# Expert routing of a two-layer block: when key lists are searched, when their sums run, and how a spilled table is fetched back

## The chip, the cores and the metric

The kernel runs on one core of one Trainium2 chip. The metric is device time in microseconds (us) of that core, from start to end of one execution; smaller is better. One core has TensorE (PE, with its weight loads shown apart as PEld), VectorE (DVE), ScalarE (ACT), GpSimd (POOL) and SyncE (SP), each with its own instruction queue, and 16 DMA engines that all queues share.

## The reference

512 tokens of width 1024 go through a first transformer block and then a second one. The change lies in the last part of the second block, a layer of 16384 experts that is addressed by product keys (PEER):

```python
q = (xn @ wq).reshape(bsz, s, PEER_HEADS, 2, PEER_HALF)
sub = jnp.einsum('bshpd,hpnd->bshpn', q, subkeys)       # 8 heads x 2 halves x 128 keys
s_top, i_top = lax.top_k(sub, PEER_TOPK)                # best 16 keys of each half
cand = (s_top[..., 0, :, None] + s_top[..., 1, None, :]) # 256 sums of pairs
best, pos = lax.top_k(cand, PEER_TOPK)                  # best 16 pairs
expert = jnp.take_along_axis(cand_idx, pos, axis=-1)    # expert = 128 * i + j
gate = jax.nn.softmax(best, axis=-1)
...
a = jax.nn.gelu(jnp.einsum('td,ted->te', xb, ub))       # ub = u_tab[expert]
y = jnp.einsum('te,ted->td', gb * a, vb)                # vb = v_tab[expert]
```

So each token picks 8 x 16 = 128 experts, and its result is the sum of their rows of `v_tab`, each weighted by its gate and by the gelu of its row of `u_tab` times the token.

## The kernel before, in words

Tokens stand in four blocks (tb = 0 to 3) of 128. The kernel treats them in two ways. For the first 320 tokens (blocks 0, 1 and half of block 2) it computes **all** 16384 experts densely on TensorE, and multiplies by a matrix of gates that is zero wherever a token did not pick the expert. For the other 192 tokens it **gathers** the rows that were picked, 1024 numbers for each of 128 tokens in one gather of 512 KB, and multiplies on VectorE. All matmuls of weights work on pairs: `unit` (L132) loads 512 KB of weights into a ring of four buffers (`raw`), ScalarE rounds it into `whi` (L138), VectorE takes the rest as `wlo` (L140), and `mm3` makes three matmuls of it (L156 to L158).

The parts in order, with the names that matter here:

- **Queries.** 16 units of `peer_wq`, four at a time (loop `c4`), give for each block and half-head 128 key scores `sub`. After every four units the scores of these four half-heads are copied out.
- **Key lists.** `top_keys` (L909) finds the best 16 of 128 keys of a half-head with five VectorE instructions (L914 to L918). Blocks 2 and 3 are searched beside the queries (list `todo`); blocks 0 and 1 after `keys` of blocks 2 and 3.
- **Keys.** `keys` (L921) adds the lists' pairs, finds the best 16 of them (L940 to L945), and looks up the key numbers. The look-up runs in four steps: ScalarE copies an operand (L968), VectorE compares and multiplies (L972, L973), and TensorE sums over eight matmuls (L976; L978 too for block 2). Its end gives the row numbers `gidx2` (block 2) and `gidx` (block 3), with which the gathers begin, or the transposed gates `sTs`.
- **Gates.** `build` (L1024) makes the gate matrix from one-hot operands: VectorE L1036, L1037, L1043, TensorE L1050, ScalarE L1051, in 48 steps. The first `N_RES` = 2 of 16 groups of it stay on chip (`gres`), the others go to DRAM (`g_dram`).
- **First half.** Beside keys and gates, 100 dense `u_block`s (L872) run on TensorE: 24 matmuls with 320 columns, gelu, result into `ab` and from there to DRAM (`a_dram`), four blocks in one store of 640 KB. The other 28 `u_block`s are left for the second half. `SPAIR` lists the 50 pairs of the first half.
- **Second half.** 64 pairs: `second` (L1160) multiplies the activations of a pair by its gates (L1170) and splits them into `wvhi` and `wvlo`; `v_block` (L1176) multiplies them by two units of `peer_v`. Activations come back from `a_dram` as `al` (two pairs a load, two buffers), gates from `g_dram` as `gl` (eight expert rows, 1536 KB a load, two buffers).
- **Gathers.** `gathered` (L887) gathers 64 times for the half of block 2, 128 times `u` rows (L899) and 128 times `v` rows (L906) for block 3, with seven buffers. 

What sets the order: `route` and `gat` are Python generators. Each `yield` names a price in us, and `advance(gen, us)` runs a generator until its prices use up the budget that the main loop gives it: `TOP_US` = 5.0 a query unit, `R_US` = 3.6 a `u_block`, `G_US` = 2.3 half a pair. A framework then places each engine's instructions in its own order within what the dependences allow, so an instruction can stand before or after its place in the program text. All loads of `raw`, `al` and `gl` are issued by SP, one after the other.

Of the kernel before, what the change touches and what calls it, by code (L numbers as in the profile page):

```python
# [39 lines left out]
N_RES = 2  # L40
# [20 lines left out]
def tile_layers(ctx: ExitStack, tc: tile.TileContext, A: dict, out: bass.AP):  # L61
# [793 lines left out]
    g_dram = drp.tile([16 - N_RES, 128, 24, 8, 16], F32, name="g_dram")  # L855
    a_dram = drp.tile([32, 128, 4, N_U], F32, name="a_dram")

# [63 lines left out]
    def keys(pr, tb):  # L921
# [41 lines left out]
        pt = bank("b")  # L963
        pt2 = bank("b") if tb == 2 else None
        for a in range(2):
            for b0 in range(0, 16, 8):
                sx = pr.tile([128, 4, 128, 2], F16, name="ohh", bufs=2).rearrange("p x i t -> p (x i t)")
                S.copy(sx.rearrange("p (b h k) -> p b h k", b=8, h=8),  # L968
                       sf[:, :, a, b0:b0 + 8].rearrange("p h b -> p b h")[:, :, :, None].to_broadcast([128, 8, 8, 16]))
                eq = pr.tile([128, 4, 128, 2], F16, name="ohl", bufs=2).rearrange("p x i t -> p (x i t)")  # L970
                e3 = eq.rearrange("p (b s) -> p b s", b=8)
                V.tensor_tensor(e3, iotab[:, b0:b0 + 8], kf[:, a, None, :].to_broadcast([128, 8, 128]), op=OP.is_equal)  # L972
                V.tensor_tensor(eq, eq, sx, op=OP.mult)  # L973
                for b in range(8):
                    l, r = (ident16, e3[:, b]) if tb == 3 else (e3[:, b], ident16)
                    T.matmul(pt[:, a * 128:(a + 1) * 128], l, r, start=(b0 + b == 0), stop=(b0 + b == 15))  # L976
                    if tb == 2:
                        T.matmul(pt2[:, a * 128:(a + 1) * 128], turn16, e3[:, b], start=(b0 + b == 0), stop=(b0 + b == 15))  # L978
# [8 lines left out]
        ge = pr.tile([128, 8, 16], F32, name="ge")  # L987
        V.tensor_tensor(ge, bv, bv[:, :, 0:1].to_broadcast([128, 8, 16]), op=OP.subtract)
        S.activation(ge, ge, AF.Exp)
        gsu = small.tile([128, 8], F32, name="gsu")  # L990
        V.tensor_reduce(gsu, ge, axis=AX.X, op=OP.add)
        V.reciprocal(gsu, gsu)
        if tb == 3:
# [9 lines left out]
        V.tensor_copy(g16, sl[:, 0])  # L1003
        V.tensor_tensor(sl[:, 1], sl[:, 0], g16, op=OP.subtract)
        for j in range(2):
# [4 lines left out]
        yield 3.0  # L1010

    def weights2():

        S.activation(zg[64:128, 0:64], ga2[64:128], AF.Gelu_apprx_tanh)
        S.activation(zg[0:64, 64:128], ga2[0:64], AF.Gelu_apprx_tanh)
        zp = bank("b")[:, 0:64]
        T.matmul(zp, zg, fold, start=True, stop=True)
        V.tensor_tensor(gT2, zp, gT2, op=OP.mult)
# [42 lines left out]
    with ExitStack() as st:  # L1061
# [24 lines left out]
        nc.scalar.dma_start(skT, A["skT"])  # L1086
        todo = []

        def routed():
            while todo or not keyed:  # L1090
                if todo:
                    yield from todo.pop(0)
                else:
                    yield 0.0
            st2.close()
            pr = pool("pr", stack=st)
            yield from keys(pr, 2)
            yield from keys(pr, 3)
            for tb in (0, 1):
                yield from top_keys(sub[tb], tb, range(16))  # L1100
            for tb in (0, 1):
                yield from keys(pr, tb)
                yield from build(pr, tb)
            while not made2:
                next(gat)
            weights2()
            yield 0.5
            yield from build(pr, 2)
# [4 lines left out]
        for c4 in range(4):  # L1113
# [10 lines left out]
            for tb in range(4):  # L1124
                S.copy(sub[tb][:, c4 * 4:c4 * 4 + 4, :], sb_[tb].rearrange("p (a n) -> p a n", a=4))
            todo += [top_keys(sub[tb], tb, range(c4 * 4, c4 * 4 + 4)) for tb in (2, 3)]
        keyed.append(True)
        for n4 in range(0, 2 * len(SPAIR), 4):
            ab = ptop.tile([128, 4, N_U], F32, name="ab", bufs=2)
            for j in range(4):  # L1130
                u_block(2 * SPAIR[(n4 + j) // 2] + j % 2, ab[:, j, :], "a")
# [5 lines left out]
            nc.scalar.dma_start(a_dram[n4 // 4], ab)  # L1137
        for _ in route:
            pass

    with ExitStack() as st:
        pv = pool("pv", stack=st)
        yb_ = [[bank("a") for _ in range(2)] for _ in range(2)] + [[bank("b") for _ in range(2)]]
        state = {"debt": 0.0}

        def first(p, j):

            if j == 0:
                if p in SPAIR:
                    n = SPAIR.index(p)  # L1150
                    if n % 2 == 0:
                        state["al"] = pv.tile([128, 4, N_U], F32, name="al", bufs=2)
                        nc.sync.dma_start(state["al"], a_dram[n // 2])
                    state[p] = state["al"][:, 2 * (n % 2):2 * (n % 2) + 2, :]
                else:
                    state[p] = pv.tile([128, 2, N_U], F32, name="av", bufs=2)
            if p not in SPAIR:
                u_block(2 * p + j, state[p][:, j, :], "b")

        def second(p):  # L1160

            i1 = 2 * p
            if i1 % 8 == 0 and i1 // 8 < N_RES:
                state["gl"] = gres[i1 // 8]
            elif i1 % 8 == 0:
                state["gl"] = pv.tile([128, 24, 8, 16], F32, name="gl", bufs=2)
                nc.sync.dma_start(state["gl"], g_dram[i1 // 8 - N_RES])
            av = state.pop(p)
# [7 lines left out]
        def v_block(i1, w):  # L1176
            vu = unit(A["peer_v"][i1 * 128:(i1 + 1) * 128, :])
            for tb in range(3):
                for hf in range(2):
                    mm3(yb_[tb][hf], w[0][:, i1 % 2, tb * 128:(tb + 1) * 128], w[1][:, i1 % 2, tb * 128:(tb + 1) * 128],  # L1180
                        vu[0][:, hf * 512:(hf + 1) * 512], vu[1][:, hf * 512:(hf + 1) * 512], i1 == 0, i1 == 127)

        for j in range(2):
            first(0, j)
        w = second(0)
        first(1, 0)
        for p in range(64):
            g_us = G_US if p in SPAIR else 1.5 * G_US
            if p < 63:
                first(p + 1, 1)  # L1190
                wn = second(p + 1)
            v_block(2 * p, w)
            state["debt"] = advance(gat, state["debt"] + g_us)
# [143 lines left out]
```

## Time and profile before

| | |
|---|---|
| median of 3 runs | 2130.1 us (2130.02 to 2134.15) |
| the profiled execution | 2130.1 us, of which the span of the trace is 2128.4 us |
| PE busy | 2048.3 us, 96% |
| DVE busy | 1575.3 us, 74% |
| queries of the expert layer | about 970 to 1048 us of the span |
| first half (100 `u_block`s, keys, gates) | about 1050 to 1485 us |
| second half (64 pairs) | about 1485 to 2118 us |

The profile is of one execution. A matmul's end is modelled, so a busy PE is not PE at its peak; what counts for PE is its idle time and the granted clock (PEclk, 1.00 is 2.4 GHz, 0.5 is 1.2 GHz). A wait is put down to the instruction that released it.

### The profile page before, as it was taken

Reading aid. Unit: us, or ns where it says so; the run is one execution under the profiler, and the core shown is the slowest. Engines: PE = TensorE matmul, PEld = TensorE weight load, DVE = VectorE, ACT = ScalarE, POOL = GpSimd, SP = SyncE. Lnnn points to the kernel's source line nnn. Section 1 sums busy time; section 2 is a strip of 40 time slices with the busy share of each in tenths; the row PEclk is TensorE's granted clock in tenths of the full one; section 3 lists DMA queues with packets and bytes.
Section 4 is the critical chain, followed back from the end, with each engine's and each line's share of the span. In section 5 each row is a group of like instructions: output and inputs, shape, how many; then the busy total and the mean of one; then the engine's idle time right before and its main releaser. Section 6 shows DMA issues by size and latency. Waiting matters only on the chain.

```text
span 2128.4 us, 29432 instructions
## 1 busy us (share of the span) xinstructions
PE 2048.3 (96%) x11104; PEld 1743.5 (82%) x11104; DVE 1575.3 (74%) x2880; ACT 821.0 (39%) x1303; POOL 524.3 (25%) x383
## 2 busy tenths in 40 slices
PE   7979999999988999999989999999999999999999
PEld 6737888888876877888889899999888878788887
DVE  6994633332259955455699999998898988899997
ACT  4364422221244342333453455555333333233332
POOL 1000100000010000000032222220575666566573
PEclk9989999999999999999999999999999999999999
DMA  5202233333222222333278899899999999999996
GB/s 190 78 21 89 80 99 98 92 98 118 81 79 80 75 84 70 109 124 99 84 282 280 288 301 359 295 364 303 373 393 410 392 404 392 410 391 410 412 405 241
DMA packets 163282, 476.47 MB, mean 224 GB/s; under 512 B 13866, under 2 KB 57266, under 8 KB 161219
## 3 DMA queue, kind: packets, MB, share of 16 engines
q1 hardware_dynamic: 67104, 259.70, 34.4%
q0 software_dynamic: 46656, 169.18, 20.8%
q10 hardware_dynamic: 49378, 45.71, 6.3%
q8 instruction: 87, 1.43, 0.3%
q14 instruction: 57, 0.46, 0.1%
HBM read 432.18 MB, written 42.09 MB: 223 GB/s over the span
## 4 chain that ended last, share of the span: by engine, by line
PE 25%; DVE 18%; issue 14%; DMA 10%; POOL 3%; ACT 1%; DVEq 0%; POOLq 0%; SPq 0%; ACTq 0%
PE bank_a L158 5%; PE bank_a L156 5%; PE bank_a L157 5%; DVE wlo L140 5%; DMA rows<-in_peer_u_dram,gidx 3%; POOL rows L883 3%; DMA rows<-in_peer_v_dram,gidx 3%; DVE rows L899 2%; DMA al<-a_dram 2%; PE bank_b L156 2%; PE bank_b L157 2%; PE bank_b L158 2%; DVE rows L891 2%; PE bank_b L1050 1%; DMA raw<-in_ut_dram 1%
## 5 line engine op out<-in xcount | busy, mean ns | idle before, releaser
L138 ACT CAST whi<-raw 128x1024 fp32r<-128x1024 f32 (+1 forms) x413 | 431.9, 1047 | 891.4 <-PE bank_a L157 327.3
L140 DVE TENSOR_TENSOR wlo<-raw,whi 128x1024 fp32r<-128x1024 f32 (+1 forms) x413 | 500.1, 1214 | 274.1 <-ACT whi L138 271.8
L156 PE MATMUL bank_a<-xhi,whi 128*128 128x320 f32 (+2 forms) x1600 | 548.2, 344 | 1.0 <-ACT xhi L152 0.8
L158 PE MATMUL bank_a<-xhi,wlo 128*128 128x320 f32 (+2 forms) x1600 | 545.1, 341 | 4.0 <-DVE wlo L140 3.7
L157 PE MATMUL bank_a<-xlo,whi 128*128 128x320 f32 (+2 forms) x1600 | 547.1, 342 | 0.6 <-DVE xlo L153 0.6
L883 POOL DMA_INDIRECT rows<-in_peer_u_dram,gidx x192 | 280.9, 1463 | 554.2 <-DVE gidx L984 145.0
L158 PEld LDWEIGHTS bank_a<-xhi,wlo 128*128 128x128 f32 x1600 | 302.2, 189 | 32.9 <-DVE wlo L140 6.0
L156 PEld LDWEIGHTS bank_a<-xhi,whi 128*128 128x128 f32 x1600 | 301.6, 189 | 29.3 <-issue 2.0
L157 PEld LDWEIGHTS bank_a<-xlo,whi 128*128 128x128 f32 x1600 | 302.7, 189 | 27.1 <-DVE xlo L153 1.6
L883 POOL DMA_INDIRECT rows<-in_peer_v_dram,gidx x128 | 207.0, 1617 | 115.2 <-DVE h L906 90.3
L164 POOL TENSOR_TENSOR rstd<-rstd,neghalf 128x1 f32<-128x1 f32 (+2 forms) x37 | 26.6, 720 | 826.2 <-DVE rstd L163 818.2
L156 PE MATMUL bank_a<-whi,wvhi 128*128 128x512 f32 x512 | 201.1, 393 | 8.2 <-ACT wvhi L152 8.1
L158 PE MATMUL bank_a<-whi,wvlo 128*128 128x512 f32 x512 | 201.4, 393 | 1.9 <-DVE wvlo L153 1.9
L157 PE MATMUL bank_a<-wlo,wvhi 128*128 128x512 f32 x512 | 200.6, 392 | 2.4 <-DVE wlo L140 2.4
L906 DVE SCALAR_TENSOR_TENSOR h<-rows,ga,h 128x1024 f32<-128x1024 f32 x128 | 164.3, 1284 | 5.2 <-DMA rows<-in_peer_v_dram,gidx 4.2
L899 DVE SCALAR_TENSOR_TENSOR rows<-rows,h 128x1024 f32<-128x1024 f32 x128 | 152.8, 1220 | 7.7 <-DMA rows<-in_peer_u_dram,gidx 7.7
L156 PEld LDWEIGHTS bank_a<-whi,wvhi 128*128 128x128 f32 x512 | 96.9, 189 | 29.1 <-ACT wvhi L152 10.2
L158 PEld LDWEIGHTS bank_a<-whi,wvlo 128*128 128x128 f32 x512 | 96.7, 189 | 25.1 <-DVE wvlo L153 5.1
L157 PEld LDWEIGHTS bank_a<-wlo,wvhi 128*128 128x128 f32 x512 | 96.8, 189 | 22.4 <-DVE wlo L140 3.2
L157 PE MATMUL bank_b<-wlo,wvhi 128*128 128x512 f32 x256 | 99.6, 389 | 0.0
L156 PE MATMUL bank_b<-whi,wvhi 128*128 128x512 f32 x256 | 99.6, 389 | 0.0
L158 PE MATMUL bank_b<-whi,wvlo 128*128 128x512 f32 x256 | 99.6, 389 | 0.0
(400 smaller groups left out, 3255.2 us busy)
## 6 DMA issues: line engine op xcount, KB each, us to landing
raw<-in_wt_dram SPq DMA_DIRECT2D x150, 512.0 KB
raw<-in_ut_dram SPq DMA_DIRECT2D x128, 512.0 KB
raw<-in_peer_v_dram SPq DMA_DIRECT2D x128, 512.0 KB
g_dram<-gt ACTq DMA_DIRECT2D x24, 896.0 KB
gl<-g_dram SPq DMA_DIRECT2D x14, 1536.0 KB
a_dram<-ab ACTq DMA_DIRECT2D x25, 640.0 KB
al<-a_dram SPq DMA_DIRECT2D x25, 640.0 KB
rows<-in_peer_u_dram,gidx POOLq DMA_INDIRECT x192
```

Source lines behind the costliest of these rows:

```text
L138: lead[0] = S.copy(hi[:, :n], raw[:, :n]).ins
L140: pace[0] = V.tensor_tensor(lo[:, :n], raw[:, :n], hi[:, :n].bitcast(F32), op=OP.subtract).ins
L156: T.matmul(o, lh, rh, start=start, stop=False)
L157: T.matmul(o, lh, rl, start=False, stop=False)
L158: T.matmul(o, ll, rh, start=False, stop=stop)
L164: G.tensor_tensor(r, r, neghalf[:, :shape[1]], op=OP.pow)
L883: G.indirect_dma_start(out=r, out_offset=None, in_=table, in_offset=bass.IndirectOffsetOnAxis(ap=idx[:, k:k + 1], axis=0))
L891: V.scalar_tensor_tensor(r, r, 1.0, hn2, op0=OP.mult, op1=OP.mult, accum_out=ga2[:, k:k + 1])
L899: V.scalar_tensor_tensor(r, r, 1.0, hn3, op0=OP.mult, op1=OP.mult, accum_out=ga[:, k:k + 1])
L906: V.scalar_tensor_tensor(h[3], r, ga[:, k:k + 1], h[3], op0=OP.mult, op1=OP.add)
L1050: T.matmul(gp[:, j, :], o_[:, g2, :, t2], oh1[:, g2, :, t2], start=o_ is ohs[0], stop=o_ is ohs[-1])
```

## The change

Four things change, all in the expert layer.

1. **Key lists.** `todo` becomes two lists, one for blocks 2 and 3 and one for blocks 0 and 1, in portions of two half-heads. What budget blocks 2 and 3 leave during the queries goes to blocks 0 and 1; the rest of these is done beside `keys` of block 3 (`zipped`).
2. **Key sums.** The matmuls of a look-up step are written one step after the VectorE instructions that make their operands, and the exponential of the gates is moved ahead of the last sums. The prices of the steps behind it are cut up.
3. **The rest of block 2's gathers** is paced by the budget (`yield next(gat)`) instead of run at once, and `weights2` is cut into steps.
4. **Fetches.** `a_dram` is stored and loaded by pairs (320 KB; five buffers of half the size, loaded four pairs ahead). `gl` is loaded in four quarters of 384 KB, one with each pair of the group before.

```diff
         pt2 = bank("b") if tb == 2 else None
+        def sums(a, b0, e3):
+            for b in range(8):
+                l, r = (ident16, e3[:, b]) if tb == 3 else (e3[:, b], ident16)
+                T.matmul(pt[:, a * 128:(a + 1) * 128], l, r, start=(b0 + b == 0), stop=(b0 + b == 15))
+                if tb == 2:
+                    T.matmul(pt2[:, a * 128:(a + 1) * 128], turn16, e3[:, b], start=(b0 + b == 0), stop=(b0 + b == 15))
+        late = None
...
                 V.tensor_tensor(eq, eq, sx, op=OP.mult)
-                for b in range(8):
-                    l, r = (ident16, e3[:, b]) if tb == 3 else (e3[:, b], ident16)
...
+                if late:
+                    sums(*late)
+                late = (a, b0, e3)
                 yield 1.4
+        ge = pr.tile([128, 8, 16], F32, name="ge")
+        V.tensor_tensor(ge, bv, bv[:, :, 0:1].to_broadcast([128, 8, 16]), op=OP.subtract)
+        S.activation(ge, ge, AF.Exp)
+        sums(*late)
+        yield 0.3
...
-        todo = []
+        todo = [[], []]
         def routed():
-            while todo or not keyed:
-                if todo:
-                    yield from todo.pop(0)
+            while todo[0] or not keyed:
+                if todo[0] or todo[1]:
+                    yield from (todo[0] or todo[1]).pop(0)
...
             yield from keys(pr, 2)
-            yield from keys(pr, 3)
-            for tb in (0, 1):
-                yield from top_keys(sub[tb], tb, range(16))
+            yield from zipped(keys(pr, 3), chain(*todo[1]))
             for tb in (0, 1):
                 yield from keys(pr, tb)
                 yield from build(pr, tb)
             while not made2:
-                next(gat)
-            weights2()
-            yield 0.5
+                yield next(gat)
+            yield from weights2()
             yield from build(pr, 2)
...
-            todo += [top_keys(sub[tb], tb, range(c4 * 4, c4 * 4 + 4)) for tb in (2, 3)]
+            for tb in (2, 3, 0, 1):
+                todo[tb < 2] += [top_keys(sub[tb], tb, range(c4 * 4 + j, c4 * 4 + j + 2)) for j in (0, 2)]
...
-        for n4 in range(0, 2 * len(SPAIR), 4):
-            ab = ptop.tile([128, 4, N_U], F32, name="ab", bufs=2)
+        for n, p in enumerate(SPAIR):
+            ab = ptop.tile([128, 2, N_U], F32, name="ab", bufs=2)
...
+        def load_a(p):
+            if p in SPAIR:
+                state[p] = pv.tile([128, 2, N_U], F32, name="al", bufs=5)
+                nc.sync.dma_start(state[p], a_dram[SPAIR.index(p)])
+        def load_g(g, k):
+            if g < N_RES:
+                state["g", g] = gres[g]
+            elif g < 16:
+                if k == 0:
+                    state["g", g] = pv.tile([128, 24, 8, 16], F32, name="gl", bufs=2)
+                sl = slice(6 * k, 6 * k + 6)
+                nc.sync.dma_start(state["g", g][:, sl], g_dram[g - N_RES][:, sl])
...
-            if i1 % 8 == 0 and i1 // 8 < N_RES:
-                state["gl"] = gres[i1 // 8]
-            elif i1 % 8 == 0:
-                state["gl"] = pv.tile([128, 24, 8, 16], F32, name="gl", bufs=2)
-                nc.sync.dma_start(state["gl"], g_dram[i1 // 8 - N_RES])
+            if i1 % 8 == 0:
+                state["gl"] = state.pop(("g", i1 // 8))
+            load_g(i1 // 8 + 1, i1 % 8 // 2)
...
+            if 5 <= p + 4 < 64:
+                load_a(p + 4)
             v_block(2 * p, w)
```

How the order of the instructions moves, at three places.

VectorE, beside the queries, just behind the first four units whose scores are out. `sub` holds scores of blocks 2 and 3, `gres` those of blocks 0 and 1; `sv` and `si` are the lists. Before, up to the next rounding rests (`wlo`):

```order
L914 MAX sv_7084<-sub_7096 128x8 x2
L915 MAX_INDEX si_7085<-sv_7084,sub_7096 128x8 x2
L916 MATCH_REPLACE sub_7096<-sv_7084,sub_7096 128x128 x2
L917 MAX sv_7084<-sub_7096 128x8 x2
L918 MAX_INDEX si_7085<-sv_7084,sub_7096 128x8 x2
L140 TENSOR_TENSOR wlo<-raw,whi 128x1024 x4
```

and now, from the last of these rows on:

```order
L918 MAX_INDEX si_7085<-sv_7084,sub_7096 128x8 x2
L917 MAX sv_7078<-gres_6485 128x8
L916 MATCH_REPLACE gres_6485<-sv_7078,gres_6485 128x128
L918 MAX_INDEX si_7079<-sv_7078,gres_6485 128x8
L917 MAX sv_7078<-gres_6485 128x8
L914 MAX sv_7078<-gres_6485 128x8
L918 MAX_INDEX si_7079<-sv_7078,gres_6485 128x8
L915 MAX_INDEX si_7079<-sv_7078,gres_6485 128x8
```

Lists of blocks 0 and 1 now stand between those of blocks 2 and 3 and the next `wlo`. Over the whole program 14 of their 32 lists (each one row of L914 that writes `sv`) move into the queries, and 18 stay in the first half.

VectorE, the end of the first half. `oh`, `ohh`, `ohl`, `ohm` are the operands of `build` for block 2, and `gres<-av` is the first multiply of the second half. Before:

```order
L140 TENSOR_TENSOR wlo<-raw,whi 128x1024
L1043 TENSOR_TENSOR ohm<-oh_13367,w2s 128x1024
L1036 TENSOR_TENSOR oh_13405<-iota_7086,sT_7069 128x1024
L1037 TENSOR_TENSOR oh_13406<-iota_7086,sT_7069 128x1024
L1043 TENSOR_TENSOR ohh<-oh_13406,w2s 128x1024
L1043 TENSOR_TENSOR ohl<-oh_13406,w2s 128x1024
L1043 TENSOR_TENSOR ohm<-oh_13406,w2s 128x1024
L140 TENSOR_TENSOR wlo<-raw,whi 128x1024 x2
L899 SCALAR_TENSOR_TENSOR rows,ga<-rows,h_70 128x1024 x2
L1170 TENSOR_TENSOR gres_6485<-av,gres_6485 128x20x32
```

and now:

```order
L140 TENSOR_TENSOR wlo<-raw,whi 128x1024
L1057 TENSOR_TENSOR ohh<-oh_13357,w2s 128x1024
L1057 TENSOR_TENSOR ohl<-oh_13357,w2s 128x1024
L1057 TENSOR_TENSOR ohm<-oh_13357,w2s 128x1024
L140 TENSOR_TENSOR wlo<-raw,whi 128x1024
L899 SCALAR_TENSOR_TENSOR rows,ga<-rows,h_70 128x1024
L140 TENSOR_TENSOR wlo<-raw,whi 128x1024 x5
L899 SCALAR_TENSOR_TENSOR rows,ga<-rows,h_70 128x1024 x3
L1190 TENSOR_TENSOR gres_6485<-av,gres_6485 128x20x32
```

The last gate operands stand two units ahead of the first multiply before, and six units now.

SP, the fetch of gate group 10 (the ninth of fourteen). Before:

```order
L134 DMA raw_16438<-in_peer_v_dram 128x1024
L1167 DMA gl_16697<-g_dram_6490 128x3072
L134 DMA raw_16468<-in_peer_v_dram 128x1024
L134 DMA raw_16503<-in_peer_v_dram 128x1024
L1153 DMA al_16929<-a_dram_6491 128x1280
L134 DMA raw_16535<-in_peer_v_dram 128x1024
```

and now:

```order
L1163 DMA al_17019<-a_dram_6491 128x640
L1173 DMA gl_16543<-g_dram_6490 128x768 x2
L134 DMA raw_16582<-in_peer_v_dram 128x1024
L134 DMA raw_16620<-in_peer_v_dram 128x1024
L1173 DMA gl_16543<-g_dram_6490 128x768 x2
L134 DMA raw_16650<-in_peer_v_dram 128x1024
```

The first two quarters stand where the whole load stood, and the last two stand two units later.

## Rows read from the trace of the kernel before

**Rows 1.** The page: the span, and TensorE over all of it (busy us, share, instructions).

```profile
span 2128.4 us, 29432 instructions
PE 2048.3 (96%) x11104; PEld 1743.5 (82%) x11104; DVE 1575.3 (74%) x2880; ACT 821.0 (39%) x1303; POOL 524.3 (25%) x383
```

**Rows 2.** Stages: stretch, length, busy us of PE, PEld, DVE, ACT, POOL; PEclk, DMA, GB/s.

```profile
970.00:1048.00 78.00, 78.00 (x391) 64.18 (x390) 40.64 (x192) 24.58 (x36) 0.00 (x0) 1.00 0.26 77
1050.00:1232.00 182.00, 170.77 (x1200) 165.10 (x1199) 178.38 (x688) 83.91 (x116) 45.76 (x37) 0.99 0.76 268
1232.00:1325.00 93.00, 91.43 (x770) 89.28 (x768) 93.00 (x200) 55.52 (x97) 20.59 (x17) 1.00 0.99 339
1325.00:1485.00 160.00, 157.53 (x1415) 153.54 (x1416) 153.17 (x232) 88.91 (x167) 29.18 (x23) 0.99 0.94 320
1485.00:2118.00 633.00, 620.01 (x2936) 524.77 (x2935) 574.62 (x653) 216.82 (x245) 392.30 (x243) 0.99 0.99 389
```

**Rows 3.** The same view, stretches of 25 us.

```profile
1075.00:1100.00 25.00, 23.18 (x179) 21.86 (x179) 21.58 (x83) 10.26 (x15) 10.11 (x10) 0.93 0.71 253
1325.00:1350.00 25.00, 24.07 (x199) 23.25 (x200) 22.13 (x35) 11.41 (x19) 3.83 (x3) 0.93 0.69 238
1750.00:1775.00 25.00, 22.52 (x93) 17.92 (x92) 24.41 (x34) 9.76 (x11) 20.53 (x13) 0.93 0.98 374
1850.00:1875.00 25.00, 19.77 (x80) 15.40 (x80) 21.56 (x20) 7.90 (x10) 13.91 (x10) 0.93 1.00 382
1975.00:2000.00 25.00, 25.00 (x114) 20.83 (x113) 23.36 (x22) 8.37 (x9) 17.41 (x11) 1.00 1.03 414
```

**Rows 4.** Waits of TensorE, 1050 to 1485 us: total us, times, longest us.

```profile
PE bank_b L976 <- DVE ohl L973: 9.3, 5, 2.5
PE bank_a L158 <- DVE wlo L140: 3.7, 7, 0.9
PE bank_b L1050 <- DVE ohh L1043: 1.2, 1, 1.2
```

**Rows 5.** Timeline of VectorE in the queries: start us, us, instruction.

```profile
995.84 0.28 DVE L915 FIND_INDEX8 si<-sv,sub 128x8 uint32<-128x128 f32 x1
...
998.17 0.29 DVE L915 FIND_INDEX8 si<-sv,sub 128x8 uint32<-128x128 f32 x1
```

**Rows 6.** Waits of all engines, 1485 to 2130 us.

```profile
DVE gl L1170 <- DMA al<-a_dram: 20.1, 5, 4.8
DVE gl L1170 <- DMA gl<-g_dram: 5.6, 3, 3.1
```

**Rows 7.** Chain of waits, one piece of 1720 to 1760 us: start us, us, what.

```profile
1726.61 13.36 DMA al<-a_dram
```

**Rows 8.** Timeline of TensorE behind two late loads; idle before and releaser in brackets.

```profile
1742.00 0.50 PE L157 MATMUL bank_a<-wlo,wvhi 128*128 128x512 f32 x1 [1.22 <-DVE wlo L140]
1752.75 0.80 PE L156 MATMUL bank_a<-whi,wvhi 128*128 128x512 f32 x1 [2.48 <-ACT wvhi L152]
1856.55 0.50 PE L157 MATMUL bank_a<-wlo,wvhi 128*128 128x512 f32 x1 [1.20 <-DVE wlo L140]
1864.35 0.50 PE L156 MATMUL bank_a<-whi,wvhi 128*128 128x512 f32 x1 [3.62 <-ACT wvhi L152]
```

**Rows 9.** Timelines of SP and VectorE around the load of gate group 10.

```profile
1834.32 0.33 SPq L1167 DMA_DIRECT2D gl<-g_dram  x1
1836.66 2.66 SPq L134 DMA_DIRECT2D raw<-in_peer_v_dram  x2
...
1845.42 1.56 DVE L1170 TENSOR_TENSOR gl<-al,gl 128x640 f32<-128x640 f32 x2 [2.20 <-DMA gl<-g_dram]
1853.34 0.82 DVE L1170 TENSOR_TENSOR gl<-al,gl 128x640 f32<-128x640 f32 x1 [4.03 <-DMA al<-a_dram]
```

**Rows 10.** The page, DMA queues: packets, MB, share of 16 engines' span.

```profile
q0 software_dynamic: 46656, 169.18, 20.8%
q10 hardware_dynamic: 49378, 45.71, 6.3%
```

More of the change, by code (lines that the diff above doesn't have):

```diff
@@ L855, in tile_layers @@
     g_dram = drp.tile([16 - N_RES, 128, 24, 8, 16], F32, name="g_dram")
-    a_dram = drp.tile([32, 128, 4, N_U], F32, name="a_dram")
+    a_dram = drp.tile([64, 128, 2, N_U], F32, name="a_dram")
     def xs4(tb):
@@ L973, in keys @@
                 V.tensor_tensor(eq, eq, sx, op=OP.mult)
-                for b in range(8):
-                    l, r = (ident16, e3[:, b]) if tb == 3 else (e3[:, b], ident16)
-                    T.matmul(pt[:, a * 128:(a + 1) * 128], l, r, start=(b0 + b == 0), stop=(b0 + b == 15))
-                    if tb == 2:
-                        T.matmul(pt2[:, a * 128:(a + 1) * 128], turn16, e3[:, b], start=(b0 + b == 0), stop=(b0 + b == 15))
-                yield 1.4
+                if late:
+                    sums(*late)
+                late = (a, b0, e3)
+                yield 1.4
+        ge = pr.tile([128, 8, 16], F32, name="ge")
[3 more added lines that the diff above has]
+        yield 0.3
+        gsu = small.tile([128, 8], F32, name="gsu")
+        V.tensor_reduce(gsu, ge, axis=AX.X, op=OP.add)
+        V.reciprocal(gsu, gsu)
         if tb == 2:
@@ L986, in keys @@
             ready.append(True)
[L987 to L992, printed above, removed]
         if tb == 3:
@@ L1004, in keys @@
         V.tensor_tensor(sl[:, 1], sl[:, 0], g16, op=OP.subtract)
+        yield 1.0
         for j in range(2):
@@ L1009, in keys @@
             S.activation(gT2, pt[:, 320:384], AF.Copy, scale=2.0 ** -14)
-        yield 3.0
+        yield 1.4
     def weights2():
+        yield 0.3
         S.activation(zg[64:128, 0:64], ga2[64:128], AF.Gelu_apprx_tanh)
         S.activation(zg[0:64, 64:128], ga2[0:64], AF.Gelu_apprx_tanh)
+        yield 0.7
         zp = bank("b")[:, 0:64]
         T.matmul(zp, zg, fold, start=True, stop=True)
+        yield 0.7
         V.tensor_tensor(gT2, zp, gT2, op=OP.mult)
@@ L1125, in tile_layers @@
                 S.copy(sub[tb][:, c4 * 4:c4 * 4 + 4, :], sb_[tb].rearrange("p (a n) -> p a n", a=4))
-            todo += [top_keys(sub[tb], tb, range(c4 * 4, c4 * 4 + 4)) for tb in (2, 3)]
+            for tb in (2, 3, 0, 1):
+                todo[tb < 2] += [top_keys(sub[tb], tb, range(c4 * 4 + j, c4 * 4 + j + 2)) for j in (0, 2)]
         keyed.append(True)
-        for n4 in range(0, 2 * len(SPAIR), 4):
-            ab = ptop.tile([128, 4, N_U], F32, name="ab", bufs=2)
-            for j in range(4):
-                u_block(2 * SPAIR[(n4 + j) // 2] + j % 2, ab[:, j, :], "a")
+        for n, p in enumerate(SPAIR):
+            ab = ptop.tile([128, 2, N_U], F32, name="ab", bufs=2)
+            for j in range(2):
+                u_block(2 * p + j, ab[:, j, :], "a")
                 if ready:
@@ L1136, in tile_layers @@
                 d1 = advance(route, d1 + R_US - (g1 if ready else 0.0))
-            nc.scalar.dma_start(a_dram[n4 // 4], ab)
+            nc.scalar.dma_start(a_dram[n], ab)
         for _ in route:
@@ L1144, in tile_layers @@
         state = {"debt": 0.0}
-        def first(p, j):
[L1148 to L1156, printed above, removed]
+        def load_a(p):
[10 more added lines that the diff above has]
+                nc.sync.dma_start(state["g", g][:, sl], g_dram[g - N_RES][:, sl])
+        def first(p, j):
+            if j == 0 and p not in SPAIR:
+                state[p] = pv.tile([128, 2, N_U], F32, name="av", bufs=2)
             if p not in SPAIR:
@@ L1181, in v_block @@
                         vu[0][:, hf * 512:(hf + 1) * 512], vu[1][:, hf * 512:(hf + 1) * 512], i1 == 0, i1 == 127)
+        load_g(0, 0)
+        for p in range(5):
+            load_a(p)
         for j in range(2):
```

## The prediction, made before the changed kernel ran

> **What bounds the kernel now.** I read the page first: TensorE (PE) is busy 96% of the span [rows 1], so what can be won is its idle time and time at the lower clock. Then the busy times by stage [rows 2]. Beside the queries PE is busy 78.0 of 78.0 us, while VectorE (DVE) has only 40.6 us of work: there is room for DVE work. In the first half it is DVE that has none: 178.4 of 182 us, 93.0 of 93, 153.2 of 160. PE is idle there for 11.2 + 1.6 + 2.5 = 15.3 us. In the second half PE, DVE and the DMA engines all stand near their limit: PE is idle 13.0 of 633 us, DVE busy 574.6, the DMA share 0.99 at 389 GB/s, and the fastest stretch shows 414 GB/s [rows 2, 3].
>
> The clock comes next. Of the stretches of 25 us, four show 0.93 [rows 3]: in each PE ran for about 25 x 0.07 x 2 = 3.5 us at 1.2 GHz instead of 2.4, which costs 1.75 us of work. In all four PE had been idle for some time before or in it (1.8, 0.9, 2.5 and 5.2 us of 25). Two lie in each half, so the ceiling is 15.3 + 3.5 = 18.8 us for the first half and 13.0 + 3.5 = 16.5 us for the second.
>
> Last the waits. In the first half PE waits 9.3 us for the operands of the key sums, in five waits, 3.7 us for `wlo` and 1.2 us for the operands of a gate matmul [rows 4]. In the second half DVE waits 20.1 us in five waits for `al` and 5.6 us in three for `gl` [rows 6]. One `al` of 640 KB stood 13.36 us between issue and landing [rows 7], and a `gl` of 1536 KB 1845.42 - 1834.32 = 11.1 us [rows 9]. Two clusters of these waits reach PE: 1.22 + 2.48 us behind 1742 and 1.20 + 3.62 us behind 1856 [rows 8], 8.5 of the 13.0 us, and both low-clock stretches of this half lie just there [rows 3].
>
> **The key lists.** Two lists that run interleaved take 998.17 - 995.84 = 2.33 us [rows 5], so one takes 1.17 us. The order shows 14 of 32 lists moved into the queries: 16.3 us of DVE. There DVE goes from 40.6 to some 57 of 78 us, which costs nothing as long as `wlo` comes before PE wants it. The worst place is the first: 14 lists in a row are 16.3 us where 8 (9.3 us) stood, so `wlo` comes 7 us later; the ring of four buffers holds up to three units of 78/12 = 6.5 us, so this is covered. Without the cover it would cost PE these 7 us once. In the first half DVE loses 16.3 us of work. If DVE alone set the time, the gain would be all of it, up to the ceiling of 18.8 us. It will be less: `advance` still gives each `u_block` the same budget, so where DVE has lists, gathers and keys it is as dense as before, only for fewer units, and what is saved shows at the end of the half, where the last gate operands now end four units earlier. Bounds for the 3.7 us of waits for `wlo`: none goes, or all. I take 3 us, nearer to all, since DVE is full in the rows and gets lighter.
>
> **The key sums.** They are written a step later, which could take away all 9.3 us. But the framework had put them elsewhere already, and the order shows only the steps of block 3 spread out, with lists between them; for blocks 2, 0 and 1 the last operands still come as late against PE as before. Bounds: 0 to 9.3 us. Block 3 is one wait of the five, at most 2.5 us; with part of another I take 3 us.
>
> **The spread gathers and weights.** The wait of 1.2 us for the first gate operands of block 2 [rows 4] goes: 1 us. Some twelve gathers of block 2 that ran at once or beside gates now come in five units without gates, which makes DVE dense there. That can give back 0 to 4 us; I take 1 us. The stores to `a_dram` go by pairs with two buffers of half the size, so ScalarE reuses a buffer after two `u_block`s instead of four. The stores go beside the work; if one landed too late, ScalarE would hold up the rounding of the next units. No row shows such a wait; I take 0, with the 2.5 us of a key-sum wait as bound.
>
> **First half:** 3 + 3 + 1 - 1 = 6 us, and with fewer long waits half of the 3.5 us of low clock is likely won: 1.7 us. Together about 7 us, between 0 and 18.8.
>
> **The fetches.** Five `al` buffers and loads four pairs ahead put the load 12 units or more ahead of its use (5 for the first four), by the order, where it stood at 3 to 15; with 13.4 us as the longest landing the 20.1 us of waits go. `gl` goes the other way. Its first quarter stands where the whole load stood, but the last stands up to two units later. In group 10 the next two units were issued at 1836.66 and 2.66 us on (the second row's length spans both issues), that is about 4.7 us after 1834.32 [rows 9]. The whole load was 2.2 us late there already. A quarter queued behind two more units lands no sooner after its issue than the whole did, at worst 4.7 us later in all. At best the smaller load lands so much earlier that nothing is lost. So this group's wait becomes 2 to 7 us. By the order five groups lie that close. With 2 to 3 us for each, 12 us are added, and DVE's waits go from 25.7 us (20.1 + 5.6) to about 17. PE lost 8.5 + 3.5 = 12 us by the 25.7, so 12 x (25.7 - 17)/25.7 = 4 us are won, between -10 and +12.
>
> More and smaller packets cost the DMA engines some time. Queue 0 took 0.208 x 16 x 2128.4/46656 = 152 ns for 3626 bytes a packet, queue 10 43.4 ns for 926 bytes [rows 10]; the line through both has 6.2 ns at zero bytes. The loads add (25 + 42) x 128 = 8576 packets: 8576 x 6.2/16 = 3.3 us of DMA time over 633 us. Two gathers fewer stand in the second half by the order (2 x 0.52 MB at 389 GB/s: 2.7 us). These offset each other.
>
> **Second half:** 4 us. **Sum:** 2130.1 - 7 - 4 = 2119 us. The profiled execution took 2130.1 us with a span of 2128.4, the same as the median.
>
> **The rivals.**
>
> *All of it is won.* The lists free DVE, the `al` waits vanish and `gl` comes in time: 18.8 us less 3 in the first half, 12 in the second, less 3: 2106 us, and at the very best 2130.1 - 18.8 - 12 = 2099. For it: DVE is full in the first half, and `al` alone makes 20.1 of the 25.7 us. Against it: the key sums' places. 15%.
>
> *The gates come late (slower).* DVE takes its instructions in order, so a multiply that waits for the last quarter holds every `wlo` and gather behind it. If not five but eight groups waited, and 6.9 us each (2.2 + 4.7), DVE would wait 55 us instead of 25.7, and at 12/25.7 us of PE for each us of DVE that is +14 us; with the first half's gain the time is 2130 + 14 - 7 = 2137 us. It decides from the point where the last quarter is issued less than some 7 us before the multiply in more than half of the groups. For it: a load of 1536 KB that stood three units earlier was late by 2.2 us. Against it: DVE has 58 us to spare in the second half, and the ring covers single waits. 12%.
>
> *The change does not do what it says.* DVE stays dense in every unit that has route work, the sums wait as now, and the DMA engines at 0.99 let the second half go no faster: 2128 us, within the noise. 20%.
>
> *Each transfer has a price of its own.* The second half moves 389 of at most 414 GB/s [rows 2, 3], so at most 633 x (1 - 389/414) = 38 us are lost to anything like it. On some 440 transfers (156 units, 39 loads of `al` and `gl`, 243 gathers) that is 0.09 us each, and 67 more make +6 us on the forecast: 2125 us. The Trainium skill (DMA: Bandwidth & Descriptors, section Anatomy of one DMA) gives a fixed cost of about 2 us for each transfer; if it took the engines, 67 more would add 134 us by that page, as an estimate. The trace speaks against that reading: 440 transfers would then need 880 us of fixed cost alone, and the half is 633 us long. The cost is hidden while many are in flight. 3%.
>
> **How the numbers follow.** The forecast, 2119 us with its own range of 2112 to 2127, has 50%. A measurement of this kernel can tell about 0.2% (4.3 us) from no change. Faster by more: nine tenths of the forecast (45%), all of the first rival (15%), a fifth of the third (4%) and some of the last (1%): 65%. Within 0.2%: 5 + 15 + 2 = 22%. Slower: 12% + 1% = 13%. The range from 2103 to 2135 leaves out the very best, and half of the slow rival.
>
> **What would show it.** Right: no `gl <- al` wait is left among DVE's waits, but waits for `gl` of 10 us or more; key-sum waits of PE between 5 and 8 us, with none in block 3; PE idle in the first half some 9 us; two or three low-clock stretches instead of four; PE still without idle time beside the queries, with DVE busy some 57 us there. Wrong: key-sum waits near zero would mean that the written order decides and that I undervalued the sums; `gl` waits above 40 us that the rival of late gates holds; PE idle unchanged in the first half that DVE's load was never what PE waited for.

## The result and the profile after

The changed kernel takes 2157.6 us (median of 4 runs, 2156.3 to 2158.7) against 2131.9 us before in the same session (4 runs): ratio 1.0118, 95% interval 1.0105 to 1.0130. It is 1.2% slower; 0.5% faster was forecast. The profiled execution spans 2157.0 us, 28.6 us more than that of before [rows 1]; the medians differ by 25.6. The page's first rows on it:

```profile
span 2157.0 us, 29621 instructions
PE 2057.0 (95%) x11104; PEld 1749.3 (81%) x11104; DVE 1575.1 (73%) x2880; ACT 821.5 (38%) x1303; POOL 533.2 (25%) x383
```

One row of PE's timeline splits the loss: the first matmul of `v_block`, behind which the second half lies. In the kernel before:

```profile
1496.92 0.40 PE L156 MATMUL bank_a<-whi,wvhi 128*128 128x512 f32 x1
```

In the changed kernel:

```profile
1499.64 0.40 PE L156 MATMUL bank_a<-whi,wvhi 128*128 128x512 f32 x1
```

Up to that row 2.7 us are lost, behind it 2157.0 - 1499.6 = 657.4 us stand against 631.5: 25.9 us lost. This split is that of two single executions, so it can be off by some us. The stages after, in the columns of [rows 2]:

```profile
970.00:1048.00 78.00, 78.00 (x386) 63.81 (x385) 57.95 (x308) 22.71 (x34) 0.00 (x0) 1.00 0.25 76
1050.00:1232.00 182.00, 172.07 (x1275) 167.31 (x1274) 177.67 (x615) 91.75 (x134) 42.35 (x35) 0.98 0.79 269
1232.00:1325.00 93.00, 92.76 (x770) 90.55 (x769) 92.27 (x201) 54.55 (x92) 20.90 (x18) 1.00 0.98 335
1325.00:1485.00 160.00, 153.25 (x1337) 150.38 (x1336) 142.41 (x210) 82.70 (x154) 36.82 (x27) 0.98 0.98 329
1485.00:2118.00 633.00, 603.78 (x2828) 509.15 (x2828) 552.16 (x634) 211.21 (x240) 392.29 (x238) 0.98 0.99 380
```

Beside the queries DVE went from 40.6 to 58.0 us and PE lost nothing, as forecast. From 1325 to 1485 us DVE lost 10.8 us of work, and yet PE's idle time rose from 2.5 to 6.8 us. In the second half PE is idle 29.2 us instead of 13.0.

The waits of PE from 1050 to 1485 us, beside [rows 4]:

```profile
PE bank_b L1064 <- ACT gt L1065: 6.7, 1, 6.7
PE bank_b L969 <- DVE ohl L982: 6.6, 3, 3.2
PE bank_a L158 <- DVE wlo L140: 3.5, 4, 1.5
```

The key sums (L969, before L976) fell from 9.3 to 6.6 us; `wlo` stayed. The first row is new, one wait in the gates (L1064, before L1050). ScalarE's timeline tells why: it stood 12.93 us, since a buffer `ab` was not stored yet.

```profile
1380.94 8.10 ACTq L1150 DMA_DIRECT2D a_dram<-ab  x1
...
1406.34 0.44 ACT L879 ACTIVATE ab<-bank_a 128x320 f32<-128x320 f32 x1 [12.93 <-DMA a_dram<-ab]
```

The store issued at 1380.94 (the issue itself took 8.10 us) landed 25.4 us later, at 1406.3. A gate store of 896 KB had been issued 2.7 us before it in the same queue, and GpSimd was issuing a gather every 1.2 to 2.3 us. By the packet records of the trace the 1792 packets of that gate store, 512 bytes each, moved from 1381 to 1405, and no packet of this store moved before 1392: it stood behind the gate store. The gates' copies out of PSUM wait behind that activation on ScalarE, and PE for them.

DVE's waits in the second half, beside [rows 6]:

```profile
DVE gl L1190 <- DMA gl<-g_dram: 51.5, 8, 11.0
DVE gl L1190 <- issue: 6.9, 2, 5.0
DVE gl L1190 <- DMA al<-a_dram: 2.7, 1, 2.7
```

The `al` waits fell from 20.1 to 2.7 us, and `gl` waits grew ninefold, from 5.6 to 51.5. Gate group 10 in SP's timeline, beside [rows 9]:

```profile
1839.85 1.29 SPq L1173 DMA_DIRECT2D gl<-g_dram  x2
1842.18 1.47 SPq L134 DMA_DIRECT2D raw<-in_peer_v_dram  x2
1843.70 0.91 SPq L1173 DMA_DIRECT2D gl<-g_dram  x2
```

The multiply that uses it, in DVE's timeline:

```profile
1857.98 1.56 DVE L1190 TENSOR_TENSOR gl<-al,gl 128x640 f32<-128x640 f32 x2 [11.04 <-DMA gl<-g_dram]
```

From the first issue to the multiply there were 11.1 us before; now there are 18.1, and the multiply waits 11.04 us instead of 2.20. In the stretches of 25 us, beside [rows 3], the clock around it fell to 0.91, and to 0.86 behind a wait of 9.6 us at 2027:

```profile
1850.00:1875.00 25.00, 17.00 (x73) 13.59 (x72) 16.95 (x17) 6.89 (x9) 8.70 (x6) 0.91 0.87 311
2025.00:2050.00 25.00, 19.35 (x72) 15.19 (x73) 22.54 (x22) 7.89 (x10) 13.43 (x9) 0.86 0.87 306
```

Behind 1485 us six such stretches have a clock of 0.95 or less; before there were two.

### The profile page after: what moved, and what is told of

The parts are those of the page before. It is cut to its first block, busy times and chain, and to the rows that moved or that the text cites. A ratio compares the mean times of both kernels' runs of the same rounds, so it can differ in the third digit from the quotient of the medians.

```text
span 2157.0 us, 29621 instructions
## 1 busy us (share of the span) xinstructions
PE 2057.0 (95%) x11104; PEld 1749.3 (81%) x11104; DVE 1575.1 (73%) x2880; ACT 821.5 (38%) x1303; POOL 533.2 (25%) x383
## 4 chain that ended last, share of the span: by engine, by line
PE 29%; DVE 19%; issue 13%; DMA 9%; ACT 1%; POOL 0%; SPq 0%; DVEq 0%; ACTq 0%; POOLq 0%
PE bank_a L156 6%; PE bank_a L158 6%; PE bank_a L157 6%; DMA gl<-g_dram 5%; DVE wlo L140 5%; DVE h L906 4%; PE bank_b L156 2%; PE bank_b L157 2%; PE bank_b L158 2%; DMA raw<-in_peer_v_dram 2%; PE bank_b L1064 1%; DVE rows L891 1%; DMA g_dram<-gt 1%; DMA raw<-in_ut_dram 1%; DVE rows L899 1%
## 5 line engine op out<-in xcount | busy, mean ns | idle before, releaser
L883 POOL DMA_INDIRECT rows<-in_peer_u_dram,gidx x192 | 290.6, 1514 | 538.9 <-DVE gidx L1000 145.6
L157 PE MATMUL bank_a<-wlo,wvhi 128*128 128x512 f32 x512 | 204.1, 399 | 15.3 <-DVE wlo L140 15.2
```

The costliest lines, as they stand in the source:

```text
L157: T.matmul(o, lh, rl, start=False, stop=False)
L883: G.indirect_dma_start(out=r, out_offset=None, in_=table, in_offset=bass.IndirectOffsetOnAxis(ap=idx[:, k:k + 1], axis=0))
```

## The experiments

Ratios are to the kernel before, measured beside each (its own medians there: 2131.9 to 2135.1 us). "Rest" is the span less the first `v_block` matmul. These two columns are of one profiled execution each, which can lie off its median: by 4.1 us above for e1, 2.5 above for e4, and 1.8 below for the kernel before in its own session. Differences of a few us in them show no more than where to look; the medians carry the argument.

| kernel | median, us | ratio, 95% interval | first `v_block` matmul | rest |
|---|---|---|---|---|
| before | 2131.9 | 1 | 1496.9 | 631.5 |
| changed | 2157.6 | 1.0118 (1.0105 to 1.0130) | 1499.6 | 657.4 |
| e1 gates whole, at the first quarter's place | 2128.1 | 0.9981 (0.9971 to 0.9991) | 1501.0 | 629.1 |
| e2 four quarters, at that place | 2143.1 | 1.0050 (1.0032 to 1.0069) | 1501.8 | 640.0 |
| e3 before + quarters | 2163.8 | 1.0154 (1.0133 to 1.0174) | 1497.2 | 663.8 |
| e4 changed, fetches of before | 2128.8 | 0.9980 (0.9968 to 0.9991) | 1493.5 | 636.1 |
| e5 as e2, cut by partitions | 2225.8 | 1.0426 (1.0409 to 1.0444) | 1499.6 | 725.2 |
| e6 changed, cut by partitions | 2261.4 | 1.0596 (1.0578 to 1.0614) | 1496.3 | 756.9 |
| e7 e1 + four store buffers | 2119.4 | 0.9928 (0.9911 to 0.9944) | 1491.1 | 626.8 |
| e8 before + key lists | 2141.2 | 1.0033 (1.0024 to 1.0043) | 1504.6 | 634.4 |
| e9 as e1, packets of 3072 bytes | 2145.9 | 1.0048 (1.0031 to 1.0065) | 1498.5 | 644.4 |
| e10 e7, sums as before | 2126.0 | 0.9957 (0.9945 to 0.9970) | 1495.4 | 628.9 |
| e11 before + `al` ahead | 2131.9 | 0.9983 (0.9972 to 0.9994) | 1502.9 | 628.0 |
| e12 e7, `al` by fours | 2117.4 | 0.9918 (0.9900 to 0.9935) | 1493.8 | 621.3 |

### Place, number or size of the gate loads (e1, e2, e3, e9)

Theory 1 is the forecast's rival: the last quarter is issued too late. Rivals to it are the DMA time of more transfers (2) and the `al` loads ahead in the queue (3).

```diff
 # e1 (e2: all four quarter loads stand under k == 0)
                 if k == 0:
                     state["g", g] = pv.tile([128, 24, 8, 16], F32, name="gl", bufs=2)
-                sl = slice(6 * k, 6 * k + 6)
-                nc.sync.dma_start(state["g", g][:, sl], g_dram[g - N_RES][:, sl])
+                    nc.sync.dma_start(state["g", g], g_dram[g - N_RES])
```

> The changed kernel, but each group's gates are fetched in one load of 1536 KB at the place of the first quarter, a whole group (four pairs) ahead of its use. Theory 1 (the last quarter of each group is issued too close to its use, behind unit loads in the same queue, and VectorE waits for it in order): the gl waits of VectorE fall from 51.5 to under 10 us and the time to 2132 us or less, a gain of at least 25 us on 2157.6. Theory 2 (more and smaller transfers cost the DMA engines time): part of the gain only, since al still comes in twice as many loads; 2140 to 2150. Theory 3 (al loaded four pairs ahead takes the queue's place from gl): no gain, 2150 to 2160, and gl is still waited for.

> The changed kernel, with the gates still in four quarter loads, but all four issued at the place of the first. The number and sizes of transfers are those of the change; only the place of three of four differs. Theory 1 (place): as with the whole load, 2132 us or less. Theory 2 (number and size): no gain, 2150 to 2160. Theory 3 (al ahead): no gain.

> The kernel before, with the gates' quarter loads of the change and nothing else of it. Theory 1: it loses what the change lost, 2150 to 2160 us, with gl waits of VectorE of 40 us or more beside the 20 us of al waits. Theory 2: 5 to 10 us slower than before at most, since only 27 loads are added. Theory 3: no loss, about 2130, since al is not loaded ahead here.

e1 won 29.5 us, so theory 3 falls: `al` is still loaded ahead there. e2 won 14.5, where theory 1 expected at least 25. e3 lost more than the whole change and keeps the `al` waits of before: the quarters alone are enough for the loss. DVE's waits for its gate multiplies from 1485 to 2160 us follow. In e3:

```profile
DVE gl L1178 <- DMA gl<-g_dram: 37.4, 6, 10.3
DVE gl L1178 <- DMA al<-a_dram: 21.2, 4, 8.2
DVE gl L1178 <- issue: 12.4, 2, 8.1
```

In e1:

```profile
DVE gl L1189 <- DMA gl<-g_dram: 10.1, 3, 5.5
```

In e2:

```profile
DVE gl L1191 <- DMA gl<-g_dram: 31.8, 7, 8.4
```

A whole group ahead in the program is not ahead in time, though. In SP's timeline of e1 group 10 is issued no earlier than before [rows 9], since both wait for one of two buffers:

```profile
1837.29 0.33 SPq L1172 DMA_DIRECT2D gl<-g_dram  x1
```

What the place changes is when the last piece goes out. It is worth half. The other half was open: number of loads, or size of packets. Whole loads are made of packets of 12288 bytes, quarters of 3072. The packet records of the trace, counted while the gates of the last 12 groups were moving (SP's queue has the unit and `al` loads too):

```
kernel   packet   SP's queue : gathers   GB/s of each   first issue to end of last packet, median
before   12288    1947 : 1930            299 : 115      10.0 us
e1       12288    2115 : 1983            299 : 115       9.1
e2        3072    7502 : 5933            203 : 202      13.1
e9        3072    7601 : 5588            209 : 193      13.4
changed   3072    (unit loads between)                   17.6
```

e9 loads the gates at once, but leaves a gap after each quarter in DRAM, so that one load is made of small packets:

```diff
-    g_dram = drp.tile([16 - N_RES, 128, 24, 8, 16], F32, name="g_dram")
+    g_dram = drp.tile([16 - N_RES, 128, 28, 8, 16], F32, name="g_dram")
...
-            nc.scalar.dma_start(g_dram[:, :, tb * 8 + ts].rearrange("g p i t -> p g (i t)"),
+            nc.scalar.dma_start(g_dram[:, :, tb * 8 + ts + (tb * 8 + ts) // 6].rearrange("g p i t -> p g (i t)"),
...
-                    nc.sync.dma_start(state["g", g], g_dram[g - N_RES])
+                    cut = lambda x: x.rearrange("p (k s) i t -> p k s i t", k=4)
+                    nc.sync.dma_start(cut(state["g", g]), cut(g_dram[g - N_RES])[:, :, :6])
```

> As the run with one whole load of gates a group ahead (2128.1 us, packets of 12288 bytes), but with a gap after each quarter of the gates in DRAM, so that the one load is made of packets of 3072 bytes, all 128 partitions at once, as the quarter loads have them. Theory A (the size of the packet decides how much of the DMA engines the gates get against the gathers): as with four quarters ahead, 2139 to 2146 us. Theory B (the number of loads decides): 2126 to 2131 us.

One load of small packets is as slow as four (2145.9 and 2143.1 us): the packet's size decides, not the number of loads. As a loss of the engines' time theory 2 falls too: the second half moves 388 GB/s in e2 as in e1 (their rows stand in the next section). What it had right is that the size of the pieces costs time.

The table shows how. While gates move, SP's queue passes 1.0 to 1.1 packets for each packet of the gathers when its gate packets are large, and 1.3 to 1.4 when they are small. So its share of the bytes goes mostly by the size of its packets. A gather packet has 4096 bytes and takes 165 ns on average; gate packets take 473 ns (12288 bytes) and 126 ns (3072). One engine's share of a gate group is 96 KB. An estimate with one packet of each queue in turn is 8 x (473 + 165) ns = 5.1 us with large packets and 32 x (126 + 165) ns = 9.3 us with small ones. The measured means from the first gate packet to the last are 5.9 us (e1) and 10.0 (e2). The Trainium skill (DMA: Bandwidth & Descriptors, section Queues, rings and completion order) says that an engine takes turns between the queues that have work, a packet of several descriptors at a time; the trace agrees on the turns, with 1947 to 1930, though 7502 to 5933 is less even. How many descriptors make a turn, none of these counts shows.

### Large packets in four loads (e5, e6)

```diff
-                sl = slice(6 * k, 6 * k + 6)
-                nc.sync.dma_start(state["g", g][:, sl], g_dram[g - N_RES][:, sl])
+                ps = slice(32 * k, 32 * k + 32)
+                nc.sync.dma_start(state["g", g][ps], g_dram[g - N_RES][ps])
```

This is e6; e5 issues all four at the first one's place.

> As the run with four quarter loads ahead (2143.1 us), but the four loads cut the gates by partitions (32 each), so that their packets stay at 12288 bytes, as in the one whole load (2128.1 us), and not 3072. In the runs so far the packets of the unit queue and of the gather queue passed about one for one while gates were moving (176 against 183 with whole loads, 638 against 628 with quarters), so that gates got some 295 GB/s with large packets and some 195 with small ones. Theory A (the size of the packet decides): 2126 to 2131 us. Theory B (the number of loads decides, each with its own price or landing): 2139 to 2146 us.

> The changed kernel with its four loads at the places that the change gave them, but cut by partitions, so that packets stay at 12288 bytes. If place and packet size add up (14.5 us for the place, 15 us for the packets, by the two runs before), 2140 to 2146 us. If the place alone decides when the last load is late, 2153 to 2159, as the changed kernel; if the packet size alone decides, 2126 to 2131.

All the theories missed, by 80 us and more. The cut changes something else: a packet of 12288 bytes that goes to 32 partitions alone takes 873 ns on average in e5 instead of 473. The engines are as busy as ever and move less, 344 GB/s where e1 and e2 have 388, the last number of these rows of the stages. e1:

```profile
1485.00:2118.00 633.00, 622.43 (x2956) 528.91 (x2955) 573.97 (x651) 218.37 (x247) 391.40 (x241) 0.99 0.99 388
```

e2:

```profile
1485.00:2118.00 633.00, 612.63 (x2911) 519.96 (x2910) 571.01 (x649) 217.20 (x248) 390.93 (x241) 0.99 1.00 388
```

e5:

```profile
1485.00:2118.00 633.00, 565.25 (x2570) 471.95 (x2569) 500.23 (x584) 192.24 (x218) 314.10 (x213) 0.95 1.01 344
```

It is the gathers that come late in e5: DVE waits 86.9 us for their rows, 6.4 in e1.

```profile
DVE rows L899 <- DMA rows<-in_peer_u_dram,gidx: 44.5, 22, 6.1
DVE h L906 <- DMA rows<-in_peer_v_dram,gidx: 42.4, 23, 6.1
```

So these two say nothing on number against size (e9 does). Why such packets take longer, and what a late place costs with large packets, was not found out.

### The first half (e4, e7, e8, e10)

> The changed kernel with both fetches, al and gl, as they were before: the key lists, key sums and spread gathers alone. My forecast for these was 7 us below before (2123 to 2125 us). By the changed kernel's trace the first half won nothing, which would give 2128 to 2134. A second half slower than that of before would mean that the first three parts cost something there too, and that the fetches are not the whole cause.

e4 is the change without its fetches. It wins 0.20%, 4.3 us, about two thirds of the 7 us forecast for the first three parts. Its profiled execution has 3.4 us less ahead of the `v_block`s and 4.6 us more behind them; DVE's waits for `al` and `gl` are 35.8 us there (25.7 before). So these parts may cost something in the second half, which e4's expectation named and one execution can't settle. The changed kernel, and e1 and e2 with it, start their `v_block`s 6 to 8 us later than e4. Up to there they differ from it only in the stores by pairs and in the first loads of the second half.

```diff
-            ab = ptop.tile([128, 2, N_U], F32, name="ab", bufs=2)
+            ab = ptop.tile([128, 2, N_U], F32, name="ab", bufs=4)
```

> The run with one whole load of gates a group ahead (2128.1 us), and four instead of two buffers of half the size for the stores to a_dram (the memory that the kernel before used). In the traces of the changed kernel ScalarE waits 12.9 us once for such a store to land, and TensorE stands 6.9 us on a gate matmul just then. If that wait costs what TensorE stood there: 2120 to 2123 us, faster than both kernels, and no wait of ab for its store is left. If something else holds TensorE at that place: 2126 to 2130 us.

With as much memory as before the wait is gone, and the buffers are all that differs from e1. e7 takes 2119.4 us, 8.7 less than e1, and beats both kernels; PE's wait in the gates shrank to 0.9 us, as its waits from 1050 to 1500 us show:

```profile
PE bank_b L969 <- DVE ohl L982: 6.6, 3, 3.2
PE bank_a L158 <- DVE wlo L140: 3.6, 5, 1.5
PE bank_b L1064 <- ACT gt L1065: 0.9, 1, 0.9
```

The edit of e8: `todo` in two lists as in the change, `zipped(keys(pr, 3), chain(*todo[1]))`, and nothing else.

> The kernel before with the key lists searched beside the queries and nothing else of the change. The prediction gave this 3 us of the 7 of the first half. If the lists carry the gain of the first three parts (4.5 us below before in the run without the fetches): 2126 to 2130 us. If they carry nothing: 2131 to 2135.

Slower by 0.33%, which neither theory had. By the code, keys that are ready earlier bring `while not made2: next(gat)` forward, to where more gathers of block 2 are still to do; they run in one lump there. PE's timeline shows it standing at the first matmul of `weights2` right behind them:

```profile
1389.91 0.66 PE L1017 MATMUL bank_b<-fold,zg 128*128 128x64 f32 x2 [5.97 <-issue]
1392.92 0.39 PE L1050 MATMUL bank_b<-oh,ohh 128*128 128x128 f16 x2 [2.36 <-DVE ohh L1043]
```

In e4, with the gathers spread, one wait of 2.8 us in the gates is left of these 8.3. So it seems that lists and spread gathers belong together, and that the spread, costed at nothing net, takes away a stall that the lists bring. This is read from two traces: e4 has the later sums as well, and no run spreads the gathers alone.

The edit of e10: `sums(a, b0, e3)` right behind its operands, and no `late`.

> The run with the whole load and four store buffers (2119.4 us), but with the key sums written right behind their operands again, as before the change. The prediction gave the later sums 3 us. If they are worth that: 2122 to 2124 us. If they are worth nothing: 2118 to 2121. In the trace of 2119.4 TensorE still stands 3.3 us at two of the sums, so I expect nothing or little.

The sums are worth about 6 us (0.9957 against 0.9928, intervals that just miss each other), more than either case expected. PE's waits for them are 10.5 us there and 6.6 in e7. Not all of it need be theirs: ScalarE waits 2.9 us for a store in e10 and not in e7.

```profile
PE bank_b L969 <- DVE ohl L981: 10.5, 4, 3.3
```

### The `al` loads (e11, e12)

> The kernel before with al by pairs, loaded four pairs ahead, and four store buffers of half the size (as much memory as before); gates, lists, sums and gathers as before. If the 20.1 us in which VectorE waits for al cost TensorE what the prediction took (12 us lost per 25.7 us of waits, so 9.4 us): 2123 to 2127 us. If these waits only move to gl, whose loads then stand behind the al loads in the same queue and with smaller packets beside them: 2131 to 2137 us.

Only 0.17% faster. The time falls into the second range, but not for its reason: the `al` waits went and the `gl` waits did not grow. DVE now stands at `wlo` instead, waiting for ScalarE's rounding (12.3 us before). Its waits from 1485 to 2160 us:

```profile
DVE wlo L140 <- ACT whi L138: 25.7, 10, 6.4
DVE gl L1169 <- DMA gl<-g_dram: 4.7, 3, 2.2
DVE gl L1169 <- DMA al<-a_dram: 2.7, 2, 2.2
```

In the second half 3.5 us are won by the profiled executions, less than half of what 20.1 us of waits were priced at, and the first half ends 6 us later. One key sum waits 5.1 us in it, where 2.5 was the longest before; why was not settled. PE's waits from 1050 to 1485 us:

```profile
PE bank_b L976 <- DVE ohl L973: 12.2, 4, 5.1
```

e12 loads `al` and stores `ab` by fours again, with three `al` buffers:

```diff
+                n = SPAIR.index(p)
+                if n % 2 == 0:
+                    state["al"] = pv.tile([128, 4, N_U], F32, name="al", bufs=3)
+                    nc.sync.dma_start(state["al"], a_dram[n // 2])
+                state[p] = state["al"][:, 2 * (n % 2):2 * (n % 2) + 2, :]
```

> The run of 2119.4 us, but with al and its stores by fours (5120-byte packets) as before the change, and three buffers in place of two, so that al is still loaded ahead. If packet size matters for al as it does for the gates: 2114 to 2118 us. If al with half the packet is in time anyway: 2118 to 2121 us, the same. Slower, 2122 or more, if loads of 640 KB in a lump hold up the unit loads behind them.

2117.4 us is the fastest time of all, 0.82% below before (its interval overlaps that of e7). The page:

```profile
span 2115.1 us, 29430 instructions
```

## Why the prediction was wrong, by its steps

**The key lists.** The place was right: 58 us of DVE beside the queries (57 forecast), free for PE. The 3 us for `wlo` did not come (3.7 to 3.5 us). What the step missed is that the lists alone bring a stall of 6 + 2.4 us at the gathers (e8). PE's idle time in the first half, forecast to fall from 15.3 to some 9 us, was 16.9; without the store's wait it is 11.2 (e7).

**The key sums.** 3 us were taken of 0 to 9.3. The waits fell by 2.7 us, and e10 puts up to about 6 us on the sums.

**Spread gathers, and the stores.** Costed at nothing net, the spread of the gathers seems to be what lets the lists pay (e8 against e4). The stores by pairs are the step that failed in this half: "ScalarE reuses a buffer after two `u_block`s instead of four" was seen, taken as 0, and bounded by 2.5 us from a key-sum wait. The row nearest to it in kind would have been a transfer's time to landing, 13.4 us [rows 7]. It measured 12.93 us of ScalarE, 6.7 us of PE and 8.7 us of time (e7). So -7 us became +2.7 in the profiled execution; e4 without these stores has -3.4.

**The fetches** are the step that failed most: -4 us became +25.9. Three sizes in it were wrong.

- "A quarter queued behind two more units lands no sooner after its issue than the whole did, at worst 4.7 us later in all." The lateness of the issue was right (median 4.3 us from the first quarter to the last). But the quarters also land slower, since packets a quarter the size get a smaller share beside the gathers: 13.1 us instead of 9.1 for the whole group at one place. Together 17.6 us instead of 10.0. By e1, e2 and the changed kernel the packets cost 15.0 us and the place 14.5.
- Five groups were to wait 2 to 3 us more each. Eight waited, up to 11.0 us. `gl` waits were forecast at some 17 us with what was left, and are 51.5.
- Of 1 us that DVE waits, PE was to lose 12/25.7 = 0.47 us. DVE's three kinds of wait grew by 61.1 - 25.7 = 35.4 us and the second half by 25.9, which is 0.73. That longer waits get past the ring's cover is likely, but was not tested; the low-clock stretches behind 1485 us went from two to six.

That `al` ahead would take its waits away was right, but they were worth little: DVE waited for the rounding instead (e11).

**The rivals.** The gates that come late is the one that happened, with its mark of `gl` waits above 40 us. Its count was near, eight waits and 55 us against eight and 51.5, but in part by luck, since it knew nothing of the packets. Its 2137 us was short because it made 14 us of these waits where the second half lost 25.9, and took 7 us off for the first half where 2.7 were lost. The rival that each transfer has its own price finds no support in e9, which has 42 loads fewer than e2 and is no faster. At 0.09 us each they would make 3.8 us, which that comparison can't exclude, but not the 25.6. The third rival's DMA engines at their limit were no protection: their share stayed 0.99, and the half still took 4% longer, since what DVE waits for is which bytes come first, not how many. The first rival's sum comes to 2105 us, not 2106. That e7 takes the 2119 us of the forecast, once the quarters and the halved store ring are undone, is luck: the kernel before took 2134.6 us beside it, so e7 won 15.2 us where 11 were forecast.

## What to carry to other kernels

Cutting an urgent load into smaller pieces can make it later, in two ways: its last piece is issued behind other work in the same in-order queue, and shorter runs per partition mean smaller packets, which here lost their share to the other busy queue. Before cutting a load or a store, look at the bytes per packet beside those of its competitors, and count in time, not in pieces, how long a buffer is held: a ring of two halves holds out half as long, here against a landing that once took 25 us. And test the parts of a change apart, since here parts worth 15 us together hid behind two faults worth 38.

## What the runs showed of the hardware

- Two busy DMA queues shared the engines more by packets than by bytes: 1947 packets passed to 1930 when the gate packets had 12288 bytes, 7502 to 5933 when they had 3072. SP's queue had 299 GB/s with the large ones, beside 115 for the gathers' 4096-byte packets, and 203 with the small ones, beside 202.
- Packets of 12288 bytes to 32 partitions took 873 ns (e5) instead of 473 with all 128 partitions in the load, and the kernel 83 us more than with four loads of all partitions (e2). The Trainium skill (DMA: Bandwidth & Descriptors, section Rules for kernel authors) says that cutting a transfer by halves of the partitions brings nothing, since both run on the same engines; here, with quarters, it cost far more than nothing.
- One store of 320 KB took 25.4 us to land: none of its packets moved in the first 11 us, behind a gate store of 512-byte packets in its queue and beside a burst of gathers.
